# Deferred transposes for rows of scales, other PSUM banks for one projection, and moved attention steps in a two-block transformer kernel

## The chip, the cores and the metric

The kernel runs on one core of a Trainium2 chip. A core has five engines with instruction queues of their own: PE (TensorE, matmuls and transposes), DVE (VectorE), ACT (ScalarE), POOL (GpSimd) and SP (which issues DMAs here). Each works through its queue in order and waits on semaphores for the others. Matmuls write to PSUM, which has eight banks per partition; everything else lies in SBUF. The metric is the device time of one execution in microseconds, the median of several runs.

## The reference

Two transformer blocks of two layers each run one after the other on one sequence of 256 tokens with 1024 features. All of it is in float32.

```
# first block: layer 0 is attention with a forget gate, layer 1 latent attention
for layer in range(2):
    h = rms_norm(x, norm_mix_g[layer])
    x = x + (fox_mixer(h, ...) if layer == 0 else mla_mixer(h, ...))
    x = x + square(relu(rms_norm(x, norm_ffn_g[layer]) @ w_up)) @ w_down
    if layer == 0: k_nope, k_rope, v = mla_shared_kv(x, ...)   # low-rank keys and values
x = rms_norm(x, final_norm_g)
# second block: gated linear attention, then a short convolution
for i in range(2):
    h = rmsnorm(x, norm_mix_g_2[i])
    x = x + (gla_mixer(h, ...) if i == 0 else short_conv_mixer(h, ...))
    x = x + conv_ffn(rmsnorm(x, norm_ffn_g_2[i]), ...)          # silu(conv(a)) * conv(u)
x = rmsnorm(x, final_norm_g_2)

# fox_mixer: 16 heads of 64, causal; cum = cumsum(log_sigmoid(h @ w_f + b_f))
p = softmax(mask(q @ k.T / 8 + cum[query] - cum[key])); ctx = p @ v; out = ctx @ w_out
# gla_mixer: 4 heads, chunks of 64; q and k scaled by exp of cumulated log gates
scores = tril((q * exp(b)) @ (k * exp(-b)).T); o = scores @ v + (q * exp(b)) @ state
```

## The kernel before

**Split products.** Every product with a weight is made of three fp32r matmuls: activations and weights are each split into a high part and the rest, and `hh*wh + hh*wl + hl*wh` is summed in one PSUM bank (`mm3`, all recorded at L339). ACT casts a raw weight tile to `wh` (L294), DVE subtracts it to give `wl` (L312); such a pair is a *unit* of two rows of 128 by 512, made up to four units ahead of its use, in a ring of five buffers. For an activation ACT casts `hh` and DVE subtracts `hl` (L509 and L512 for norm inputs, L732 and L733 for a head pair's context).

**Ticks and what hangs on them.** The builder writes the projections one after the other and counts a tick after every group of matmuls (three of 512 columns, or six of 256; about 0.65 us). `after(n, fn)` puts a piece of other work off by n ticks, with most n in the table `DLY`. A side generator, `attend`, issues the attention visits between the groups. Its tables `FOX` and `MLA` have one entry per step: the ticks to wait, then the visits to weigh (p times v), to transpose (`pT`), and to start (logits, mask and maximum on DVE at L716, exponentials on ACT at L697; the normalisation at L704 and L707 follows eight ticks later or when the transposes need it). A fox visit is one pair of heads over all 256 queries, 8 in all; visits 4 to 7 read the second half of q, k and v. A scheduler then sets the final order of each engine's queue.

**Banks.** PSUM is parted into four accumulator banks (`acc`), three working banks (`up`) and one for transposes (`tp`); each pool is a ring. Before the output projection of fox attention needs all four accumulators, its visits borrow `acc` banks; after that (`late` is True) they take `up` banks.

**Rows of scales.** A projection whose result stands transposed (features on partitions) needs the norm's scales along the free axis. `make_row` (L137 to L149) makes such a row: DVE spreads two columns wide (L144), PE transposes them into the `tp` bank (L523), ACT copies that to `rowb` (L148). DVE's `by_row` (L416, and L419 with a factor) then multiplies the projection by it when it empties the bank.

**Linear attention.** `gla` projects v and the gate inputs, then keys (into `acc` banks), queries (into `up` banks), gates `g` (into `up` banks). While the gates' projection runs, the side generator `core` starts with the scores, which PE forms out of qT and kT; DVE multiplies the decays into qT at L1240, one half of the heads at a time.

## Time and profile before

| | |
|---|---|
| runs | 1104.15, 1104.34 and 2274.76 us; median 1104.34 us |
| the profiled execution | 1104.49 us, of which the span of instructions is 1102.7 us |
| busy share of the span | PE 99%, weight loads 91%, DVE 73%, ACT 55%, POOL 3% |
| mean granted TensorE clock | 0.997 |
| DMA | 207.3 MB, 188 GB/s in the mean |

The page gives the busy time of each engine, the span in 40 slices, the chain of work that ended last, and the costliest groups of instructions. The other views are taken from the same trace: a timeline lists an engine's instructions with the start, the length and, in brackets, an idle time ahead of them with what ended it; the waits view sums such idle times. Lines are those of the kernel before. In the changed kernel they are five higher behind `make_row` (in which L144 becomes L145 and L148 becomes L151), so that L339 there is L344, L419 is L424, and so on.

### The profile page before, as it was taken

To read this page: it belongs to the slowest core of one execution; us is meant where nothing else is said; L and a number is where in the kernel's file an instruction comes from. 1 tells how busy PE (TensorE), PEld (TensorE's weight loads), DVE (VectorE), ACT (ScalarE), POOL (GpSimd) and SP (SyncE) were. 2 spreads that over 40 slices of the span, in tenths; PEclk is the share of its full clock that TensorE was granted. 3 is DMA by queue.
4 is the path that set the end of the run, shared out by engine and by line. 5 is a ranking of instruction groups with operands and counts; after the bars stand their busy time and mean duration, and the time that the engine had idled before them with its cause. 6 is when DMAs were issued, how large, how long until landed. Compare 5 with 4: busy or idle time off the path is not lost.

```text
span 1102.7 us, 19201 instructions
## 1 busy us (share of the span) xinstructions
PE 1087.3 (99%) x7769; PEld 1003.4 (91%) x7769; DVE 801.4 (73%) x1200; ACT 609.2 (55%) x927; POOL 30.4 (3%) x55
## 2 busy tenths in 40 slices
PE   9999999999999999999999999999999999999997
PEld 7987999999988999999897899999999999999996
DVE  6687756556687766555788578787787768987786
ACT  6466655445665555545664556555555446565563
POOL 1000000000000000000010000000000000000001
PEclk9999999999999999999999999999999999999998
DMA  9844466655563566665555354566665664657551
GB/s 335 298 165 145 162 195 206 210 193 173 142 207 128 172 192 204 206 200 192 194 180 183 108 178 155 179 197 217 201 220 193 197 204 153 189 194 224 188 166 74
DMA packets 137801, 207.30 MB, mean 188 GB/s; under 512 B 10528, under 2 KB 65008, under 8 KB 137712
## 3 DMA queue, kind: packets, MB, share of 16 engines
q1 hardware_dynamic: 136576, 203.89, 56.8%
q10 hardware_dynamic: 1136, 2.17, 0.5%
q8 instruction: 61, 1.00, 0.4%
q14 instruction: 28, 0.23, 0.1%
HBM read 204.97 MB, written 1.07 MB: 187 GB/s over the span
## 4 chain that ended last, share of the span: by engine, by line
PE 87%; DVE 7%; ACT 2%; DMA 1%; issue 1%; SPq 0%; ACTq 0%; DVEq 0%
PE up L339 52%; PE acc L339 33%; DVE wl L312 2%; DMA raw<-fox_w_in 1%; ACT wh L294 1%; PE acc L523 1%; PE tp L523 1%; ACT p L697 1%; DVE p L716 1%; DVE x L602 0%; DVE p L707 0%; PE tp L533 0%; DVE tmp L1365 0%; DVE pT L725 0%; DVE kT L1232 0%
## 5 line engine op out<-in xcount | busy, mean ns | idle before, releaser
L312 DVE TENSOR_TENSOR wl<-raw,wh 128x1024 fp32r<-128x1024 f32 (+2 forms) x373 | 452.3, 1219 | 223.4 <-ACT wh L294 222.4
L294 ACT CAST wh<-raw 128x1024 fp32r<-128x1024 f32 (+2 forms) x373 | 388.8, 1043 | 381.7 <-PE up L339 253.1
L339 PE MATMUL up<-hh,wh 128*128 128x256 f32 x1564 | 431.7, 276 | 0.0
L339 PE MATMUL up<-hh,wl 128*128 128x256 f32 x1564 | 430.1, 275 | 0.0
L339 PE MATMUL up<-hl,wh 128*128 128x256 f32 x1564 | 429.4, 275 | 0.0
L339 PEld LDWEIGHTS up<-hh,wh 128*128 128x128 f32 x1564 | 300.1, 192 | 2.9 <-issue 1.5
L339 PEld LDWEIGHTS up<-hh,wl 128*128 128x128 f32 x1564 | 300.1, 192 | 0.9
L339 PEld LDWEIGHTS up<-hl,wh 128*128 128x128 f32 x1564 | 299.8, 192 | 0.3 <-DVE hl L512 0.2
L339 PE MATMUL acc<-wh,hh 128*128 128x512 f32 (+1 forms) x606 | 227.4, 375 | 0.2 <-DVE mx L716 0.2
L339 PE MATMUL acc<-wh,hl 128*128 128x512 f32 (+1 forms) x606 | 225.1, 371 | 0.1
L339 PE MATMUL acc<-wl,hh 128*128 128x512 f32 (+1 forms) x606 | 224.8, 371 | 0.0
L339 PEld LDWEIGHTS acc<-wh,hl 128*128 128x128 f32 x606 | 114.5, 189 | 15.4 <-DVE hl L1374 0.5
L339 PEld LDWEIGHTS acc<-wh,hh 128*128 128x128 f32 x606 | 114.6, 189 | 15.0 <-DVE mx L716 0.6
L339 PEld LDWEIGHTS acc<-wl,hh 128*128 128x128 f32 x606 | 114.7, 189 | 13.4
L1365 DVE SCALAR_TENSOR_TENSOR tmp<-tmp,vecs,tmp 128x255 f32<-128x255 f32 x192 | 78.0, 479 | 15.2 <-ACT tmp L1363 15.2
L339 PE MATMUL up<-wh,hh 128*128 128x512 f32 (+4 forms) x142 | 52.2, 370 | 1.8 <-DVE tmp L419 1.8
L339 PE MATMUL up<-wl,hh 128*128 128x512 f32 (+4 forms) x142 | 49.9, 352 | 0.2 <-DVE wl L312 0.2
L339 PE MATMUL up<-wh,hl 128*128 128x512 f32 (+4 forms) x142 | 49.8, 353 | 0.1
L1363 ACT ACTIVATE tmp<-tmp,vecs 128x256 f32<-128x256 f32 x96 | 40.9, 496 | 0.0
L1373 ACT CAST hh<-tmp 128x512 fp32r<-128x512 f32 x58 | 34.1, 619 | 8.3 <-DVE tmp L1418 8.3
L1374 DVE TENSOR_TENSOR hl<-tmp,hh 128x512 fp32r<-128x512 f32 x58 | 38.3, 685 | 0.0
L339 PEld LDWEIGHTS up<-wh,hh 128*128 128x128 f32 x142 | 26.8, 189 | 8.1 <-issue 5.5
(205 smaller groups left out, 769.8 us busy)
## 6 DMA issues: line engine op xcount, KB each, us to landing
raw<-ffn_w_up SPq DMA_DIRECT2D x176, 256.0 KB, 4.2
raw<-ffn_w_up SPq DMA_DIRECT2D x32, 1024.0 KB, 5.3
raw<-ffn_w_down SPq DMA_DIRECT2D x32, 1024.0 KB, 5.0
raw<-ffn_w_down SPq DMA_DIRECT2D x44, 512.0 KB, 6.6
raw<-sc_w_in SPq DMA_DIRECT2D x12, 1024.0 KB, 5.3
raw<-fox_w_in SPq DMA_DIRECT2D x10, 1024.0 KB, 9.7
raw<-gla_w_in SPq DMA_DIRECT2D x10, 1024.0 KB, 5.0
raw<-fox_w_out SPq DMA_DIRECT2D x4, 1024.0 KB, 5.2
```

The costliest lines, as they stand in the source:

```text
L294: self.last_hi = nc.scalar.copy(hi[:, :kn, :w], self.raws[r][:, k:k + kn])
L312: self.last_wl = nc.vector.tensor_tensor(out=u.lo[:, :kn, :w], in0=self.raws[r][:, k:k + kn], in1=u.hi[:, :kn, :w].bitcast(F32), op=ALU.su ...
L339: self.nc.tensor.matmul(out, lhsT, rhs, start=start, stop=stop, skip_group_check=True)
L523: self.nc.tensor.transpose(tp[:, i * P:(i + 1) * P], src[:, i * P:(i + 1) * P], self.ident)
L697: self.nc.scalar.activation(out=p[:, o:o + n], in_=p[:, o:o + n], func=AF.Exp, scale=scale, bias=nm[:, j:j + 1], accum_out=sm[:, j:j + 1])
L716: self.nc.vector.tensor_tensor_reduce(out=p[:, o:o + n], in0=lgs[h][:, w], in1=bias(h)[:, w], scale=1.0, scalar=NEG, op0=ALU.add, op1=ALU. ...
L1363: nc.scalar.activation(out=out, in_=z, func=AF.Copy, scale=w[:, 2:3])
L1365: nc.vector.scalar_tensor_tensor(out=out[:, d:], in0=z[:, :S - d], scalar=w[:, 2 - d:3 - d], in1=out[:, d:], op0=ALU.mult, op1=ALU.add)
L1373: nc.scalar.copy(hi, src)
L1374: nc.vector.tensor_tensor(out=lo, in0=src, in1=hi.bitcast(F32), op=ALU.subtract)
```

## The change

Four things are edited. `make_row` still issues the DVE copy at once, but puts the two transposes and the ACT copy off by three ticks; a set `asked` keeps a row from being made twice. `gla` projects the queries into accumulator banks. In `FOX` the first gap is 6 instead of 8, the seventh 6 for 5, the eighth 5 for 4, the ninth 7 for 5; in `MLA` the seventh is 6 for 7 and the last 3 for 2. In `DLY`, entry 0 (from the gain's multiplication of a norm input to its split) is 4 for 5, entry 1 (from an addition to x to the transposes of the next norm's input) 5 for 4, and entry 6 (the cumulation of the forget gates) 8 for 6.

```diff
--- before.py
+++ after.py
@@ -121,7 +121,7 @@
 
 
     def __init__(self, kb, tile):
-        self.kb, self.tile, self.ok, self.rows = kb, tile, set(), {}
+        self.kb, self.tile, self.ok, self.rows, self.asked = kb, tile, set(), {}, set()
 
     def set(self, *cols):
         self.ok.update(cols)
@@ -134,24 +134,29 @@
         self.wait(i[1].start, i[1].stop)
         return self.tile[i]
 
-    def make_row(self, c, tp=None):
-
-        if c in self.rows:
+    def make_row(self, c, tp=None, gap=3):
+
+        if c in self.asked:
             return
+        self.asked.add(c)
         kb, nc = self.kb, self.kb.nc
         self.wait(c, c + 2)
         wide = kb.tmp_tile()
         nc.vector.tensor_copy(wide[:, :S].rearrange("p (t n) -> p t n", t=2),
                               self.tile[:, c:c + 2].unsqueeze(2).to_broadcast([P, 2, P]))
-        tp = kb.transpose4(wide, 2, tp if tp is None else lambda: tp)
-        row = kb.small.tile([P, S], F32, tag="rowb", name=kb.name("rowb"), bufs=2)
-        nc.scalar.copy(row, tp[:, :S])
-        self.rows[c] = row
+
+        def turn():
+            bank = kb.transpose4(wide, 2, None if tp is None else lambda: tp)
+            row = kb.small.tile([P, S], F32, tag="rowb", name=kb.name("rowb"), bufs=2)
+            nc.scalar.copy(row, bank[:, :S])
+            self.rows[c] = row
+
+        kb.after(gap, turn)
 
     def row(self, c, n=2):
 
         while c not in self.rows:
-            if c in self.ok and c + 1 in self.ok:
+            if c in self.ok and c + 1 in self.ok and c not in self.asked:
                 self.make_row(c)
             else:
                 self.kb.force()
@@ -1344,7 +1349,7 @@
             self.after(DLY[21], lambda: self.prep(yy, t, list(range(4 * j, 4 * j + 4)), [(y, None)]))
 
         self.proj_T(h, 8, ev_k, self.acc_tile)
-        self.proj_T(h, 8, ev_q)
+        self.proj_T(h, 8, ev_q, self.acc_tile)
         while self.q:
             self.force()
         self.side = core()
@@ -1682,14 +1687,14 @@
 
 
 
-FOX = [(8, [], [], [0]), (6, [], [], [1]), (6, [], [0], [2]), (6, [0], [1], [3]), (6, [1], [2], [4]), (6, [2], [3], [5]),
-       (5, [3], [4], [6]), (4, [], [5], [7]), (5, [4], [6], []), (5, [5], [7], []), (5, [6], [], []), (2, [7], [], [])]
+FOX = [(6, [], [], [0]), (6, [], [], [1]), (6, [], [0], [2]), (6, [0], [1], [3]), (6, [1], [2], [4]), (6, [2], [3], [5]),
+       (6, [3], [4], [6]), (5, [], [5], [7]), (7, [4], [6], []), (5, [5], [7], []), (5, [6], [], []), (2, [7], [], [])]
 MLA = [(0, [], [], [0]), (4, [], [], [1]), (7, [], [0], []), (5, [0], [1], []), (3, [1], [], [2]), (4, [], [], [3]),
-       (7, [], [2], []), (4, [2], [3], []), (2, [3], [], [])]
+       (6, [], [2], []), (4, [2], [3], []), (3, [3], [], [])]
 
 WARM = (10, 3)
 
-DLY = [5, 4, 11, 2, 2, 3, 6, 4, 6, 2, 11, 4, 6, 2, 6, 8, 5, 1, 1, 2, 2, 5, 1, 3, 2, 1, 3, 4, 8, 2, 2, 2, 1, 1, 1, 1]
+DLY = [4, 5, 11, 2, 2, 3, 8, 4, 6, 2, 11, 4, 6, 2, 6, 8, 5, 1, 1, 2, 2, 5, 1, 3, 2, 1, 3, 4, 8, 2, 2, 2, 1, 1, 1, 1]
 
 
 @with_exitstack
```

The order of the instructions on POOL and SP is the same in both kernels. On the others it differs in many places, three of which are shown. First DVE's queue behind the masked logits of visit 3, before the change (`nm` is the shift of that visit, `rc` and `p` its normalisation, `kT_206` the second half of the keys):

```order
L794 SCALAR_TENSOR_TENSOR nm_923<-mx_918,ctok 128x4 [waits DVE_49]
L795 TENSOR_TENSOR nm_923<-nm_923,ctok 128x4 [waits DVE_49]
L312 TENSOR_TENSOR wl_938<-raw_594,wh_937 128x2x512 [waits Activation_49]
L416 TENSOR_TENSOR kT_206<-up_751,rowb_285 128x512 [waits PE_49]
L704 RECIPROCAL rc_1035<-sm_926 128x4 [waits Activation_49]
L416 TENSOR_TENSOR kT_206<-up_752,rowb_285 128x512 [waits PE_49]
L707 TENSOR_SCALAR p_917<-p_917,rc_1035 128x128 [waits DVE_49]
L707 TENSOR_SCALAR p_917<-p_917,rc_1035 128x256
L707 TENSOR_SCALAR p_917<-p_917,rc_1035 128x128
L707 TENSOR_SCALAR p_917<-p_917,rc_1035 128x256
```

And the same place now:

```order
L799 SCALAR_TENSOR_TENSOR nm_911<-mx_906,ctok 128x4 [waits DVE_49]
L800 TENSOR_TENSOR nm_911<-nm_911,ctok 128x4 [waits DVE_49]
L709 RECIPROCAL rc_1029<-sm_914 128x4 [waits Activation_49]
L712 TENSOR_SCALAR p_905<-p_905,rc_1029 128x128 [waits DVE_49]
L712 TENSOR_SCALAR p_905<-p_905,rc_1029 128x256
L712 TENSOR_SCALAR p_905<-p_905,rc_1029 128x128
L712 TENSOR_SCALAR p_905<-p_905,rc_1029 128x256
L317 TENSOR_TENSOR wl_944<-raw_594,wh_943 128x2x512 [waits Activation_49]
L421 TENSOR_TENSOR kT_206<-up_757,rowb_334 128x512 [waits PE_49]
L421 TENSOR_TENSOR kT_206<-up_758,rowb_334 128x512 [waits PE_49]
```

The two evacuations of the keys stood around the reciprocal; they now stand behind the whole normalisation and a `wl`.

The second place is PE's queue at visit 7, the last to start. Before, with the transposes of visit 5 ending and the logits in `acc` banks:

```order
L533 MATMUL tp_1198<-ident,p_1087 128x64
L533 MATMUL acc_1199<-ident,p_1087 128x64
L339 MATMUL acc_1214<-kT_206,qT_204 128x128
L339 MATMUL acc_1215<-kT_206,qT_204 128x128 [waits DVE_49]
L339 MATMUL acc_1214<-kT_206,qT_204 128x256
L339 MATMUL acc_1215<-kT_206,qT_204 128x256
L339 MATMUL acc_1234<-wh_975,hh_890 128x512 [waits DVE_49]
L339 MATMUL acc_1234<-wl_976,hh_890 128x512
L339 MATMUL acc_1234<-wh_975,hl_891 128x512
L339 MATMUL acc_1235<-wh_975,hh_890 128x512 [waits DVE_49]
```

Now (`up_1212` takes half of the transposes, `up_1227` and `up_1228` the logits of the two heads; the first group of the output projection, `acc_1197`, stands just ahead of these rows):

```order
L538 MATMUL tp_1211<-ident,p_1084 128x64
L538 MATMUL up_1212<-ident,p_1084 128x64
L344 MATMUL up_1227<-kT_206,qT_204 128x128 [waits Activation_49]
L344 MATMUL up_1227<-kT_206,qT_204 128x256
L344 MATMUL acc_1198<-wh_1020,hh_878 128x512
L344 MATMUL acc_1198<-wl_1021,hh_878 128x512
L344 MATMUL up_1228<-kT_206,qT_204 128x128 [waits Activation_49]
L344 MATMUL up_1228<-kT_206,qT_204 128x256
L344 MATMUL acc_1198<-wh_1020,hl_879 128x512
```

The logits of the two heads are now parted by matmuls of the output projection, and each of them waits for ACT. What ACT has to do there, now (`up_1018` and `up_1019` hold the two token blocks of the second half of v; the exponentials are those of visit 6):

```order
L621 ACTIVATE v_208<-up_1018,rs_117 128x512 [waits PE_49]
L702 ACTIVATE p_1159,sm_1168<-p_1159,nm_1165 128x128 [waits DVE_49,Activation_49]
L702 ACTIVATE p_1159,sm_1168<-p_1159,nm_1165 128x256
L702 ACTIVATE p_1159,sm_1168<-p_1159,nm_1165 128x128
L702 ACTIVATE p_1159,sm_1168<-p_1159,nm_1165 128x256
L621 ACTIVATE v_208<-up_1019,rs_117 128x512 [waits PE_49]
```

In the kernel before, the same six operations stand in the same order. The bank of `up_1228` is the one that `up_1019` held.

The third place is PE's queue at the end of the queries' projection in linear attention, before:

```order
L339 MATMUL up_6213<-hh_5862,wl_6177 128x256
L339 MATMUL up_6213<-hl_5863,wh_6176 128x256
L339 MATMUL up_6338<-wh_6214,hh_5748 128x512 [waits Activation_49]
L339 MATMUL up_6338<-wl_6215,hh_5748 128x512 [waits DVE_49]
L339 MATMUL up_6338<-wh_6214,hl_5749 128x512
L339 MATMUL up_6339<-wh_6214,hh_5748 128x512 [waits DVE_49,PE_49]
L339 MATMUL up_6339<-wl_6215,hh_5748 128x512
L339 MATMUL up_6339<-wh_6214,hl_5749 128x512
```

And now, up to the first scores (`up_6361`):

```order
L344 MATMUL acc_6213<-hh_5862,wl_6177 128x256
L344 MATMUL acc_6213<-hl_5863,wh_6176 128x256
L344 MATMUL up_6338<-wh_6214,hh_5748 128x512 [waits Activation_49]
L344 MATMUL up_6338<-wl_6215,hh_5748 128x512 [waits DVE_49]
L344 MATMUL up_6338<-wh_6214,hl_5749 128x512
L344 MATMUL up_6339<-wh_6214,hh_5748 128x512 [waits PE_49]
L344 MATMUL up_6339<-wl_6215,hh_5748 128x512
L344 MATMUL up_6339<-wh_6214,hl_5749 128x512
```

Eight rows further on:

```order
L344 MATMUL up_6361<-qT_5765,kT_5766 64x64 [waits DVE_49,PE_49,Activation_49]
L344 MATMUL up_6361<-qT_5765,kT_5766 64x64 x3
L344 MATMUL up_6338<-wh_6244,hh_5748 128x512 [waits Activation_49]
L344 MATMUL up_6338<-wl_6245,hh_5748 128x512
L344 MATMUL up_6361<-qT_5765,kT_5766 64x64 [waits DVE_49]
L344 MATMUL up_6361<-qT_5765,kT_5766 64x64 x3
L344 MATMUL up_6338<-wh_6244,hl_5749 128x512
```

The queries' own rows name `acc` banks, and the start of the second gate bank (`up_6339`) waits for no DVE instruction any more. The scores stand nine matmuls behind that start in both kernels, with the same waits.

## Rows read from the trace of the kernel before

**Rows 1.** The page: span, and busy time of TensorE (share of the span).

```profile
span 1102.7 us, 19201 instructions
...
PE 1087.3 (99%) x7769; PEld 1003.4 (91%) x7769; DVE 801.4 (73%) x1200; ACT 609.2 (55%) x927; POOL 30.4 (3%) x55
```

**Rows 2.** The page: the chain that ended last, its shares by engine.

```profile
PE 87%; DVE 7%; ACT 2%; DMA 1%; issue 1%; SPq 0%; ACTq 0%; DVEq 0%
```

**Rows 3.** Timeline of PE around 590: start us, duration us, engine, line, operation, [wait].

```profile
590.25 0.28 PE L339 MATMUL up<-hl,wh 128*128 128x256 f32 x1
590.37 0.38 PE L339 MATMUL up<-wh,hh 128*128 128x512 f32 x1
...
590.80 0.38 PE L339 MATMUL up<-wh,hl 128*128 128x512 f32 x1
592.93 0.45 PE L339 MATMUL up<-wh,hh 128*128 128x512 f32 x1 [1.75 <-DVE tmp L419]
...
595.04 0.45 PE L339 MATMUL up<-qT,kT 128*64 128x64 f32 x8
...
596.05 0.45 PE L339 MATMUL up<-qT,kT 128*64 128x64 f32 x8
```

**Rows 4.** Timeline of DVE in the same stretch.

```profile
589.76 2.36 DVE L312 TENSOR_TENSOR wl<-raw,wh 128x1024 fp32r<-128x1024 f32 x2
592.03 1.08 DVE L419 SCALAR_TENSOR_TENSOR tmp<-up,rowb 128x256 f32<-128x256 f32 x3
593.03 0.69 DVE L1240 TENSOR_TENSOR qT<-tmp,qT 128x512 f32<-128x512 f32 x1
...
593.96 1.22 DVE L312 TENSOR_TENSOR wl<-raw,wh 128x1024 fp32r<-128x1024 f32 x1
595.09 0.69 DVE L1240 TENSOR_TENSOR qT<-tmp,qT 128x512 f32<-128x512 f32 x1
```

**Rows 5.** Timeline of PE at the first row copy and at visits 4 and 7.

```profile
21.66 0.44 PE L523 MATMUL tp<-ident,tmp 128*128 128x128 f32 x2 [0.44 <-DVE tmp L144]
...
75.22 0.87 PE L339 MATMUL acc<-kT,qT 64*128 64x128 f32 x8
...
91.10 0.27 PE L533 MATMUL tp<-ident,p 64*128 64x64 f32 x1 [0.64 <-DVE pT L725]
...
93.62 0.48 PE L339 MATMUL acc<-wh,hh 128*128 128x512 f32 x1 [0.20 <-DVE mx L716]
```

**Rows 6.** Timeline of DVE during the visits.

```profile
64.03 0.28 DVE L716 CUSTOM_DVE_ANT_0 p<-acc,bias 128x128 f32<-128x128 f32 x1
...
73.21 0.68 DVE L416 TENSOR_TENSOR kT<-up,rowb 128x512 f32<-128x512 f32 x1
...
...
74.82 1.00 DVE L707 TENSOR_SCALAR p<-p,rc 128x128 f32<-128x128 f32 x4
75.73 1.22 DVE L312 TENSOR_TENSOR wl<-raw,wh 128x1024 fp32r<-128x1024 f32 x1
...
77.67 0.28 DVE L716 CUSTOM_DVE_ANT_0 p<-acc,bias 128x128 f32<-128x128 f32 x1
...
90.96 0.28 DVE L716 CUSTOM_DVE_ANT_0 p<-acc,bias 128x128 f32<-128x128 f32 x1
```

**Rows 7.** Timeline of PE in latent attention.

```profile
316.00 0.41 PE L523 MATMUL acc<-ident,tmp 128*128 128x128 f32 x2 [0.42 <-DVE tmp L144]
...
358.90 0.45 PE L339 MATMUL up<-pT,v 128*128 128x256 f32 x1 [0.50 <-DVE pT L725]
```

**Rows 8.** Timeline of DVE in latent attention.

```profile
355.93 2.36 DVE L312 TENSOR_TENSOR wl<-raw,wh 128x1024 fp32r<-128x1024 f32 x2
358.20 0.55 DVE L725 COPY pT<-tp 128x384 f32<-128x384 f32 x1
```

**Rows 9.** Timeline of ACT at visit 6: first exponential, and the evacuation of v.

```profile
92.64 0.40 ACT L697 ACTIVATE p<-p,nm 128x128 f32<-128x128 f32 x1 [2.10 <-DVE nm L795]
...
94.41 0.67 ACT L616 ACTIVATE v<-up,rs 128x512 f32<-128x512 f32 x1
```

## The prediction

> **What bounds the kernel now.** I read the page first. TensorE is busy for 1087.3 of 1102.7 us [rows 1], and the chain of work that ended last is 87% PE, 7% DVE and 2% ACT [rows 2]. So PE is the bound nearly everywhere, and a change that only reorders work can win no more than what PE stands still. That is 15.4 us in all, 1.4% of the time, a part of it start-up that this change does not touch. The matmuls themselves stay the same in number and shape. What counts, then, is single waits: I read the views of waits of PE and the timelines of PE, DVE and ACT in the stretches that the edits touch, and held the order of the changed program against them. The profiled execution took 1104.49 us, 0.15 over the median of 1104.34, so the two are one number here.
>
> In the timelines a reader is to see how far a PE row starts after the one ahead of it. A 256-wide matmul takes PE 0.11 us and a 512-wide one 0.215 when nothing is in the way (590.25 to 590.37, and the two from 590.37 to 590.80, in [rows 3]). Anything beyond that is a wait.
>
> **Linear attention's queries in accumulator banks.** Today the gate projection needs two `up` banks, the queries hold two of the three, and PE waits 1.75 us for DVE's L419 to empty one: the start goes from 590.80 to 592.93, 2.13 us where 0.21 would do, 1.9 lost [rows 3]. In accumulator banks the queries hold no `up` bank, and the order shows that the second gate bank no longer waits for DVE. The accumulators are empty early enough: DVE's order has their evacuation (L1200) well ahead of the wl that the queries' projection needs. So this wait goes. But what is late next? Three gate groups on, PE's scores read qT, which L1240 writes in two halves. DVE runs without a pause from 589.76 (two wl, then L419, L1240, L419, another wl, the second L1240), and ends the second half at 595.09 + 0.69 = 595.78 [rows 4]. Its order there is the same after the change. PE does the second half of the scores at 596.05 today [rows 3]. It would reach that point about 594.1, wait 0.6 us at the first half (ready 593.03 + 0.69 = 593.72) and some 1.3 us at the second, and go on at about 595.8. So of 1.9 us only 0.25 is left as gain. Just ahead, the row copy of the norm and one `hl` come later in PE's order, which spares PE up to about half a microsecond and lets the DVE chain start that much sooner, since it is fed by PE's projections; I take 0.45 of it. Together -0.7, with ends at -0.25 (no head start for DVE) and -2.4 (the wait goes in full).
>
> The Trainium skill ("Perfetto Trace Analysis", section "Optimizing Tensor Performance", Matmuls) says that independent groups of matmuls should rotate through different PSUM banks, so that the evacuation of one overlaps the matmuls of the next. By that rule the 1.9 us would all be won, and the sum would be 1.65 lower. The row agrees that the bank is what is waited for today, but it shows nothing of what comes after; the DVE rows say that the data are late too.
>
> **Rows of scales three groups later.** `make_row` now emits only the DVE copy, and its two transposes and ACT copy come three groups on. Nothing is added to any engine but two or three small rows. Where PE waited for the copy it no longer does. At 316.00 in the latent-attention layer a transpose waited 0.42 us for L144 [rows 7]; the order has it now behind the rotary transposes, and the row is wanted only when kT is evacuated, later still in DVE's order, so I take -0.45 (bounds -0.6 and 0, should the kT evacuation come to wait for the row). At 21.66, at the start, PE waited 0.44 us for L144 [rows 5]; there the head transposes of the first queries move up in its place, and they wait for ACT. I count +0.25 there, because they end no sooner. If ACT were in time the 0.44 would be a gain; both ends are small.
>
> **Latent attention's table.** The seventh gap goes from 7 to 6 and the last from 2 to 3: the third visit's transposes come one group earlier, and the weighing after them stays. Today PE waits 0.50 us at 358.90 for the pT copy [rows 7], which DVE starts at 358.20 behind two wl [rows 8]. Now the transposes come three 512-wide matmuls, 0.65 us, sooner, and in DVE's order the copy stands ahead of the second wl, so it ends 1.1 us earlier. The wait goes: -0.55 with the step from one kind of matmul to the next.
>
> **Forget-gate attention's table** is the large item. Visits 0 to 3 come 12 matmuls of 0.11 us, 1.34 us, earlier in PE's order, visits 4 and 5 three earlier, the last four steps three groups later. But a visit is a chain over DVE and ACT: four masked rows with their maxima (ISA in the order, 1.1 us), two small ones for the shift (0.4), four exponentials on ACT (1.8: 92.64 to 94.41 [rows 9]), a reciprocal and four normalisations (1.15), a wl (1.15), hl and pT (0.8): 6.65 us, which is the period between 77.67 and 90.96 [rows 6] (two periods). That chain, not PE, sets visits 4 to 7.
>
> - Visit 2's masked rows start at 64.03 now [rows 6]. Their logits come 1.34 us earlier, but DVE is full there with masks, qT and wl, and I put them at 63.05.
> - To visit 3: hl, pT and a wl all stand between, about 6.9 us: 69.95.
> - To visit 4: today DVE does the two kT evacuations from 73.21 on, before the normalisations at 74.82 and the wl at 75.73 [rows 6]. Now both stand behind reciprocal, normalisations and wl: kT is ready at about 76.2 and 76.8. PE gets to visit 4's logits at about 74.5 (75.22 before [rows 5]) and waits some 1.6 us. The chain needs 7.85: 77.8 (77.67 before).
> - To visit 5 one wl more stands ahead of the shift: 7.7, 85.5. To visit 6: 6.65, 92.15, where it was 90.96 [rows 6]. The chain is 1.2 late.
> - Visit 7: PE waited 0.64 for pT at 91.10 and 0.20 for an accumulator at 93.62 [rows 5]. A group of the output projection now stands ahead of the transposes, and the logits have `up` banks of their own, since the switch `late` is already set: both waits go. But the second logits bank is the one that holds the second half of v, and ACT empties it (L616) behind the exponentials of visit 6, at 94.41 + 0.67 today [rows 9], so at about 95.6 + 0.67 = 96.3. PE would be there at about 93.6 and waits 2.7 us.
>
> Behind that wait PE has done two matmuls (0.43 us) more than at 93.62 before, and an estimated 0.35 us of logits follow (half of a visit's, from the 0.87 of its eight rows at 75.22): 96.3 + 0.35 - 0.43 - 93.62 = **+2.6 us**. The earlier waits, the +0.25 of the start among them, are swallowed in it, as PE waits here for the chain. Bounds: if DVE keeps visit 6 at its old time, +1.4; if the 1.34 us of head start carries through, about 0; if the chain is a further 1 us late, +3.6. I take 2.6, as every DVE duration in it is from a row.
>
> The last four steps come later, so the last context parts do too: by my times the last hl ends about 0.4 us before PE reads it. This costs nothing while that holds.
>
> **Norm inputs.** With DLY[0] 4, DLY[1] 5 the transposes of x come one group later and the splits as much earlier after them. DVE's adds and hl end when they did, and that is what PE waits for at the five norm places; I count 0 (bounds -0.5 and +0.3). DLY[6], the cumulation two groups later, stands at the same place in PE's order: 0.
>
> **Sum.** +2.6 (visits, with the start) - 0.45 (row) - 0.55 (latent) - 0.7 (linear attention) = +0.9 on 1104.49: 1105.4, and on the median of 1104.34 **1105.2 us**. That is no change: a measurement of this kernel can tell about 2%, 22 us, from no change.
>
> **Rivals.**
> - *The bank was all* (chance 0.2): qT is ready sooner than I think, because DVE's chain starts sooner. The whole 1.9 and the 0.45 are won: 1105.2 - 1.65 = 1103.55. For it speaks that the chain is fed by PE; against it that DVE has no pause in [rows 4].
> - *The visits gain* (0.25): the head start of visits 0 to 3 outlives the extra wl and kT rows on DVE, and v's bank is empty 1.2 to 2.6 us sooner. Then the visits cost between +1.4 and 0: 1104.0 to 1102.6, middle 1103.3. With the bank as well, 1101.6. Against it: the order puts kT behind the normalisations.
> - *The tail breaks* (0.15), the one on the slower side: the last part of the context is late. It decides when the chain is more than 0.4 us later than I have it; each further microsecond is then a wait ahead of the last matmuls of the output projection, besides the one for v's bank. With the chain 1 us late: +1 at v's bank and +0.6 in the tail, 1106.8.
> - My forecast has 0.4: 1104.1 to 1106.2.
>
> The range, 1101.8 to 1107.0, takes in all four but for the far ends: both gaining rivals at once below it, a tail over 1 us late above it. Faster by over 2% would need more than all of PE's 15.4 us, 0.01; slower by over 2%, 22 us of new waits where I find 5, 0.01; the rest is 0.98.
>
> **What would show it.** Right: PE waits at the score matmuls (`up<-qT,kT`) near 593 to 596 for L1245, not for L424; a wait near 74 to 76 at `acc<-kT,qT` for L421; one of 2 to 3 us near 93 to 96 at `up<-kT,qT`, with ACT's L621 behind the exponentials; no wait at the pT weighing near 358 nor at L528 near 315. Wrong: visit 6's masked rows at or before 91, no wait at 74, or scores that start at 594 without a wait. What would upset the total is a new wait in the repeated layers, where I count none.

## The result and the profile after

The changed kernel takes **1110.38 us** (median of five runs, 1108.69 to 1112.18) where the kernel before takes 1104.31 (median of five): a ratio of 1.0055 with an interval of 1.0044 to 1.0067, or 6.1 us more. That is no change by the bound of 2%, but it is outside the range that was given (1101.8 to 1107.0), and nearly seven times the +0.9 that was forecast. The profiled execution took 1110.24 us, against 1104.49 before, 5.75 more.

The page of the changed kernel, the lines that answer to [rows 1] and [rows 2]:

```profile
span 1108.5 us, 19206 instructions
...
PE 1089.9 (98%) x7769; PEld 1005.5 (91%) x7769; DVE 801.5 (72%) x1200; ACT 609.4 (55%) x927; POOL 30.4 (3%) x55
...
PE 86%; DVE 9%; ACT 2%; issue 1%; DMA 1%; POOL 0%; SPq 0%; ACTq 0%; DVEq 0%; POOLq 0%
```

The matmuls are the same 7769. PE stands still for 18.6 us instead of 15.4, and it is *busy* for 2.6 us longer, which the same matmuls should not be. The second is the unusual part: these 2.6 us are not waits.

The view of PE's waits, whole kernel (engine, line, who is waited for: us in total, times, longest):

```profile
PE up L344 <- DVE hl L517: 2.5, 3, 1.4
PE up L344 <- DVE qT L1245: 1.6, 2, 0.9
...
PE acc L344 <- DVE kT L421: 1.3, 1, 1.3
PE up L344 <- ACT v L621: 1.3, 1, 1.3
```

The waits of before for the bank [rows 3] and for L144 [rows 5, 7] are gone from it. In their place stand waits for `qT`, `kT` and `v`, which were forecast, and at the top one for `hl`, which was not.

Since both kernels do the same matmuls, one can ask at each point how much later the changed kernel reaches the same amount of matmul work. I call this the **lag**; it is worked out from the starts of all 7769 matmuls of both traces, and tells where the time goes. Times of the kernel before are on the left:

| stretch (us of before) | lag at its start and end | change | forecast |
|---|---|---|---|
| start, first row copy, to 58 | 0 to -0.4 | -0.4 | } |
| forget-gate visits, 58 to 122 | -0.4 to +4.1 | +4.5 | } +2.6 |
| latent attention, 295 to 400 | +4.1 to +3.7 | -0.4 | -1.0 |
| norm input of linear attention, 535 to 570 | +3.7 to +5.5 | +1.8 | 0 |
| linear attention, 570 to 620 | +5.5 to +5.3 | -0.2 | -0.7 |
| three norm places behind it, near 653, 831, 918 | +5.3 to +5.8 | +0.45 | 0 |

The sum, +5.8, is the difference of the two profiled executions. (The lag does not move in the stretches left out.) Two more norm places lie inside these stretches, near 121 (0.17 of the second line) and near 375 (0.12, which the third line's gain has to make good). Two things make the miss: the start and the visits together reach +4.0 ahead of the norm place at 121, some 1.4 us more than was forecast, and the norm input of linear attention, counted at nothing, cost 1.8.

**The visits.** The timelines of PE, DVE and ACT, with one wait ahead of visits 4 and 7 (start us, duration, engine, line, operation, [wait]):

```profile
59.22 0.35 PE L344 MATMUL up<-hh,wh 128*128 128x256 f32 x1 [0.72 <-DVE rc L709]
...
75.81 0.93 PE L344 MATMUL acc<-kT,qT 64*128 64x128 f32 x8 [1.33 <-DVE kT L421]
...
93.87 0.38 PE L344 MATMUL acc<-wl,hh 128*128 128x512 f32 x1
95.53 1.31 PE L344 MATMUL up<-kT,qT 64*128 64x128 f32 x4 [1.28 <-ACT v L621]
96.77 0.79 PE L344 MATMUL acc<-wh,hl 128*128 128x512 f32 x1
97.36 0.63 PE L344 MATMUL acc<-wh,hh 128*128 128x512 f32 x1
97.79 0.63 PE L344 MATMUL acc<-wl,hh 128*128 128x512 f32 x1
98.21 0.63 PE L344 MATMUL acc<-wh,hl 128*128 128x512 f32 x1
98.64 0.63 PE L344 MATMUL acc<-wh,hh 128*128 128x512 f32 x1
99.07 0.52 PE L344 MATMUL acc<-wl,hh 128*128 128x512 f32 x1
99.42 0.38 PE L344 MATMUL acc<-wh,hl 128*128 128x512 f32 x1
```

```profile
75.08 1.28 DVE L421 TENSOR_TENSOR kT<-up,rowb 128x512 f32<-128x512 f32 x2
```

```profile
94.81 0.67 ACT L621 ACTIVATE v<-up,rs 128x512 f32<-128x512 f32 x1
```

Both forecast waits are there, and a third at 59.22 that the forecast does not have. The third costs little in this execution: the lag is -0.36 at 58 and -0.26 at 64. By the starts, PE stands 1.5 us for `kT` at 75.81, and 1.45 at 95.53 for the bank of `v` (from 93.87 to 95.53 is 1.66 us, where 0.215 would do). But behind the second wait the matmuls of 512 columns start 0.43 us apart (97.36, 97.79, 98.21, 98.64, 99.07) and not 0.215 as in [rows 3]. The view by windows says why (window: sum, busy of PE, PEld, DVE, ACT, POOL, granted TensorE clock as a share, DMA):

```profile
92.00:94.00 2.00, 2.00 (x20) 1.19 (x18) 1.44 (x8) 0.95 (x5) 0.00 (x0) 1.00 0.95 289
94.00:96.00 2.00, 0.72 (x5) 0.47 (x4) 1.02 (x7) 2.00 (x7) 0.00 (x0) 0.98 0.53 204
96.00:98.00 2.00, 2.00 (x6) 1.17 (x5) 1.57 (x9) 0.79 (x2) 0.41 (x1) 0.50 0.00 0
98.00:100.00 2.00, 2.00 (x7) 1.65 (x7) 1.07 (x2) 0.16 (x1) 0.72 (x2) 0.67 0.04 8
100.00:102.00 2.00, 2.00 (x11) 1.75 (x10) 1.08 (x1) 2.00 (x7) 0.00 (x0) 1.00 0.00 0
```

TensorE's granted clock fell to 0.50 behind the wait, that is to 1.2 GHz, its lower level, near 95.9, and was back at 2.4 near 99.3 (worked out from the 0.98 and the 0.67 of the windows at its two ends). The logits and the six matmuls behind them take 3.89 us from 95.53 to 99.42, where 2.2 would do at the full clock (0.85 for the logits and 0.32 for the matmul behind them, as the same rows take in a trace without the fall, and five of 0.215): 1.65 us more. This is the greater part of the 2.6 us of extra busy time.

**The norm input of linear attention.** PE's rows, and then DVE's queue, after:

```profile
550.53 0.38 PE L344 MATMUL up<-wh,hl 128*128 128x264 f32 x1 [0.61 <-DVE hl L517]
...
559.89 0.38 PE L344 MATMUL up<-wh,hl 128*128 128x264 f32 x1 [1.41 <-DVE hl L517]
```

```profile
557.93 1.30 DVE L1141 TENSOR_SCALAR x<-x,rs 128x512 f32<-128x512 f32 x3 [1.14 <-POOL rs L568]
559.16 0.68 DVE L517 TENSOR_TENSOR hl<-tmp,hh 128x512 fp32r<-128x512 f32 x1
```

and DVE's queue there before:

```profile
552.02 0.68 DVE L512 TENSOR_TENSOR hl<-tmp,hh 128x512 fp32r<-128x512 f32 x1
...
554.17 1.31 DVE L1136 TENSOR_SCALAR x<-x,rs 128x512 f32<-128x512 f32 x3 [0.86 <-POOL rs L563]
```

Before, the last `hl` stood ahead of the scaling of x, and DVE's wait for POOL's norm statistic cost nothing. Now `hl` stands behind the scaling; DVE waits 1.14 us for POOL and scales for 1.3 before it writes the `hl` that PE has been waiting for.

**Linear attention.** The bank wait of [rows 3] is gone, and the scores wait for `qT` instead, where before they did not wait:

```profile
599.39 0.45 PE L344 MATMUL up<-qT,kT 128*64 128x64 f32 x8 [0.74 <-DVE qT L1245]
...
601.37 0.45 PE L344 MATMUL up<-qT,kT 128*64 128x64 f32 x8 [0.89 <-DVE qT L1245]
```

**Latent attention.** The 0.42 us for the row copy [rows 7] is gone, and this came a little later, a wait for the split of a norm input:

```profile
321.24 0.38 PE L344 MATMUL up<-hl,wh 128*128 128x256 f32 x1 [0.52 <-DVE hl L517]
```

### The profile page after: what moved, and what is told of

It is laid out like the page before. It is cut to its first block, busy times and chain, and to the rows that moved or that the text cites. A ratio compares the mean times of both kernels' runs of the same rounds, so it can differ in the third digit from the quotient of the medians.

```text
span 1108.5 us, 19206 instructions
## 1 busy us (share of the span) xinstructions
PE 1089.9 (98%) x7769; PEld 1005.5 (91%) x7769; DVE 801.5 (72%) x1200; ACT 609.4 (55%) x927; POOL 30.4 (3%) x55
## 4 chain that ended last, share of the span: by engine, by line
PE 86%; DVE 9%; ACT 2%; issue 1%; DMA 1%; POOL 0%; SPq 0%; ACTq 0%; DVEq 0%; POOLq 0%
PE up L344 50%; PE acc L344 33%; DVE wl L317 3%; PE acc L528 1%; DMA bias<-rows 1%; ACT wh L299 1%; ACT p L702 1%; DVE p L721 1%; PE tp L528 1%; DVE p L712 0%; DVE hl L517 0%; DVE x L607 0%; DVE tmp L1370 0%; ACT tmp L621 0%; PE acc L1612 0%
## 5 line engine op out<-in xcount | busy, mean ns | idle before, releaser
L344 PE MATMUL up<-hh,wh 128*128 128x256 f32 x1532 | 423.1, 276 | 0.7 <-DVE rc L709 0.7
L344 PE MATMUL up<-hl,wh 128*128 128x256 f32 x1532 | 420.9, 276 | 0.5 <-DVE hl L517 0.5
L344 PE MATMUL up<-hh,wl 128*128 128x256 f32 x1532 | 420.8, 275 | 0.0
L344 PEld LDWEIGHTS up<-hh,wh 128*128 128x128 f32 x1532 | 294.0, 192 | 4.3 <-issue 2.4
L344 PEld LDWEIGHTS up<-hh,wl 128*128 128x128 f32 x1532 | 294.0, 192 | 0.9
L344 PEld LDWEIGHTS up<-hl,wh 128*128 128x128 f32 x1532 | 293.6, 192 | 1.1 <-DVE hl L517 0.9
L1370 DVE SCALAR_TENSOR_TENSOR tmp<-tmp,vecs,tmp 128x255 f32<-128x255 f32 x192 | 78.0, 478 | 15.4 <-ACT tmp L1368 15.4
```

The lines of the kernel that those rows point to most:

```text
L344: self.nc.tensor.matmul(out, lhsT, rhs, start=start, stop=stop, skip_group_check=True)
L1370: nc.vector.scalar_tensor_tensor(out=out[:, d:], in0=z[:, :S - d], scalar=w[:, 2 - d:3 - d], in1=out[:, d:], op0=ALU.mult, op1=ALU.add)
```

## The experiments

Two questions were open: what the visits cost without the rest (and whether the fall of the clock belongs to them), and whether the norm inputs alone make the wait for `hl`. Each part was therefore done alone or undone. Medians of the kernel before beside these runs were 1104.28 in the first two sets (27 and 30 runs) and 1104.42 in the third (21).

### The visits alone, and the change without them

`fox_only` is the kernel before with the new table of the visits:

```diff
-FOX = [(8, [], [], [0]), (6, [], [], [1]), ... (5, [3], [4], [6]), (4, [], [5], [7]), (5, [4], [6], []),
+FOX = [(6, [], [], [0]), (6, [], [], [1]), ... (6, [3], [4], [6]), (5, [], [5], [7]), (7, [4], [6], []),
```

> The kernel before with the new table of forget-gate visits (FOX) and nothing else of the change. Theory A (the table alone builds the waits for kT near 74 and for v's bank near 94, and TensorE's granted clock then falls behind the second one as in the changed kernel's trace): +4.4 us, about 1108.7, with the PE interval of 512-wide matmuls doubled for some 2 us after the wait near 94. Theory B (the waits are the table's, but the fall of the clock needs the other edits too): +2.2, about 1106.5, no slow stretch.

Measured: 1107.82 us (six runs, 1106.58 to 1108.48), ratio 1.0031 (1.002 to 1.0043). The same kernel was run again in the third set, as `fox_again`:

> The kernel before with the new FOX table, once more, beside the next run on the same chip: the spread of its executions is looked for. Theory A (behind the 1.45 us wait for v's bank TensorE's granted clock falls in some executions and not in others): two clusters, near 1107.0 and 1.2 to 1.5 us higher. Rival (the spread is noise): one cluster within 0.9 us, as the kernel before has.

Measured: 1108.23 (1107.0, 1107.03, 1108.23, 1108.43, 1108.65), ratio 1.0032 (1.0019 to 1.0044). The eleven runs of this one program fall into two groups: five at 1106.58 to 1107.56, six at 1108.09 to 1108.65. Both profiles are of the lower group. The wait for `v` is the same there as after the whole change, but no fall follows:

```profile
94.34 0.38 PE L339 MATMUL acc<-wl,hh 128*128 128x512 f32 x1
96.01 0.92 PE L339 MATMUL up<-kT,qT 64*128 64x128 f32 x4 [1.29 <-ACT v L616]
96.86 0.48 PE L339 MATMUL acc<-wh,hl 128*128 128x512 f32 x1
97.18 0.38 PE L339 MATMUL acc<-wh,hh 128*128 128x512 f32 x1
```

```profile
94.00:96.00 2.00, 0.72 (x3) 0.30 (x2) 0.55 (x3) 2.00 (x9) 0.00 (x0) 1.00 0.77 297
96.00:98.00 2.00, 1.99 (x9) 1.55 (x10) 1.97 (x13) 1.26 (x2) 0.33 (x1) 1.00 0.00 0
```

From 90 to 114 the lag rises by 1.05 in `fox_only` and in `fox_again`, and by 2.7 in the changed kernel: the fall costs 1.65, as in the rows above. At 114 it stands at +2.8, where the changed kernel's is +4.0, which is 1.2 more and not 1.65, because the changed kernel came to 90 with 0.45 less: the wait near 59 is 0.72 there, and 1.27 and 0.86 in the two profiles here. The upper group lies 1.3 above the lower (means of 1108.34 and 1107.04). So the forecast of +2.6 was right for an execution without the fall, and the fall adds 1.3 by the groups and 1.65 by the rows.

That the upper group are executions with a fall is inferred, since no profile fell on one. Besides the size, the mean granted clock of each execution speaks for it. In all 78 executions of the kernel before it is 0.997 to 0.999. The two traces with a fall (the changed kernel's and that of `best2`, below) have 0.996, and so have twelve more executions of all kernels here, each in the upper group of its kernel. The six of the upper group here have 0.9968 in the mean, the five of the lower 0.9978. Single values, rounded to 0.001, do not part the groups: five of the six show 0.997. Of the changed kernel's five executions the shortest, 1108.69, has 0.998 and the others 0.996 or 0.997, so it is likely one without a fall; at 4.4 above the kernel before it too lies outside the forecast range. So neither theory of `fox_only` came out as it stood: the table alone makes the waits, and the fall, if it is what parts the groups, comes in some executions only.

`no_fox` is the changed kernel with the old table of visits:

> The changed kernel with the old FOX table. Theory A: 4.3 us of the 6 go, about 1106.0, and no slow stretch of TensorE before 110 us. Rival (the waits only move to the output projection of this layer or later): more than 1108.

Measured: 1106.56 (eleven runs, 1105.58 to 1108.0), ratio 1.0023 (1.0014 to 1.0032). The lag is +0.2 at 295, -0.2 at 535, +1.6 at 570 and +1.6 at the end. By the medians the visits make 3.8 of the 6.1 us; the rest of the change costs 2.3 us where I had it gain 1.7. The profiled execution, at 1106.09, is 0.5 below the median; the three longest, 1107.54 to 1108.0, are at a granted clock of 0.996, so a fall, which this kernel's waits for `qT` can bring as well (see `best2`), is likely in them. The old visits with entry 6 of `DLY` at 8 leave the lag at 0 from 58 to 118, so that entry cost nothing there.

### Visit 7 with the old banks

`fox_v7` is the changed kernel with visit 7 started one group earlier, when it still takes its logits from accumulator banks, so that nothing waits for `v`:

```diff
-       (6, [3], [4], [6]), (5, [], [5], [7]), (7, [4], [6], []), ...
+       (6, [3], [4], [6]), (4, [], [5], [7]), (7, [4], [6], []), ...
```

> The changed kernel with the eighth gap of FOX 4 in place of 5: visit 7 starts a group earlier, while its logits still have accumulator banks, so nothing waits for the bank that holds the second half of v. Theory A (that wait, and the fall of the clock behind it, are the dearest part of the table): no wait near 94 and no slow stretch there, 2.7 us less than the changed kernel, about 1107.7; the 1.5 us for kT near 74 stay. Rival (the softmax chain on DVE and ACT sets the end of the layer whatever bank is used): within 0.7 of 1110.4.

Measured: 1107.37 (eight runs, 1106.86 to 1107.71), ratio 1.0026 (1.0016 to 1.0036): 3.0 us less than the changed kernel for one number. The waits of PE between 55 and 125 are these, without `v`:

```profile
PE acc L344 <- DVE kT L421: 1.4, 1, 1.4
PE up L344 <- DVE nm L800: 1.2, 1, 1.2
```

The granted clock is 1.00 in every window from 92 to 102, and the runs lie within 0.9 us instead of in two groups. From 90 to 114 the lag falls by 0.9, where it rises by 1.05 in `fox_only` (the late bank, no fall) and by 2.7 in the changed kernel (both). So by the traces the late bank costs 1.9 us, of which 1.45 are the wait itself, and the fall behind it another 1.65. That is 3.6 where the medians differ by 3.0; in the profiles 0.8 of it is not seen at the end, since `fox_v7` came to 90 with that much more lag (its wait near 60 is 1.2 us and not 0.72, and its start 0.3 later).

### A longer occupation of the bank

To see whether a longer wait makes the fall certain, `fox_long` adds to `fox_only` one more evacuation of the same bank by ACT, into a scratch tile, ahead of that of `v`:

```diff
             def f(t, ps):
+                if t:
+                    junk = self.small.tile([P, 512], F32, tag="junk", name=self.name("junk"), bufs=1)
+                    self.scaled(junk, ps, rs[:, t:t + 1])
                 self.scaled(v[i][:, t], ps, rs[:, t:t + 1])
```

> The same with one more evacuation of v's second block on ACT (into a scratch tile, used by nobody) ahead of the one that PE waits for: the wait for v's bank grows by 0.57 us to about 2.0. Theory A (a longer wait makes the fall of the clock the rule): +0.6 by the wait and the upper cluster in most executions, median near 1109. Rival (the fall does not hang on this wait): +0.6 on the median of the run beside it and the same spread.

Measured: 1108.56 (1106.82, 1107.3, 1108.56, 1108.95, 1109.07), ratio 1.0036 (1.0022 to 1.005). This decides nothing. The bank came free later, but the order had moved and PE did two more matmuls first, so that it stood idle for 1.45 us by the timeline instead of 1.29, and the groups are as before (two executions at 1106.82 and 1107.3 with a granted clock of 0.997 and 0.998, three at 1108.56 to 1109.07 with 0.996).

### The norm inputs

`dly01_only` is the kernel before with entries 0 and 1 of `DLY` changed:

```diff
-DLY = [5, 4, 11, ...
+DLY = [4, 5, 11, ...
```

> The kernel before with DLY[0] 4 and DLY[1] 5 and nothing else. Theory A (the second low half of the linear attention's input then stands in DVE's queue behind operations that wait for POOL's norm statistics): a wait of about 1.4 us at the hl matmul near 555 and one of 0.6 near 547, +1.8 there and +0.1 at each later norm: about 1106.3. Rival (the later row copy makes that wait): within 0.4 of 1104.3.

Measured: 1106.71 (ten runs, 1105.97 to 1107.21), ratio 1.0023 (1.0014 to 1.0032), so **+2.4 us** from a term that was counted at 0. Its waits between 540 and 570, where the kernel before has none on PE:

```profile
PE up L339 <- DVE hl L512: 2.0, 2, 1.4
```

The lag goes from +0.5 at 535 to +2.15 at 570, then in steps of 0.17 near 653, 831 and 918: the three late steps of the changed kernel are here too, as are those near 121 (0.17) and 375 (0.12).

`dly0_only` changes entry 0 alone:

> The kernel before with DLY[0] 4 (splits one group sooner after the gain) and the transposes of x where they were. Theory A (the loss of the pair is the transposes' later place, which puts the last hl behind DVE operations that wait for POOL): no loss, the 0.3 us wait for hl near 552 goes, about 1103.9. Rival (the sooner split is what reorders DVE): 1106 or more.

Measured: 1105.65 (eleven runs, 1105.43 to 1105.92), ratio 1.0011 (1.0002 to 1.002), +1.4. My theory, that the earlier split alone would do no harm, fell. DVE's order had turned over with that entry alone:

```profile
554.30 1.31 DVE L1136 TENSOR_SCALAR x<-x,rs 128x512 f32<-128x512 f32 x3 [1.14 <-POOL rs L563]
555.53 0.68 DVE L512 TENSOR_TENSOR hl<-tmp,hh 128x512 fp32r<-128x512 f32 x1
```

This `hl` stood at 552.02 before, ahead of the scaling. Of the 2.4 us, 1.4 are thus entry 0; the rest comes with entry 1, as a second wait for `hl` near 547 and the five steps of 0.12 to 0.17 at the other norm places, of which entry 0 alone shows none.

### The rows of scales

`row_only` is the kernel before with the new `make_row`:

> The kernel before with the deferred transposes of rows and nothing else. Theory A (what is won at 304, 315 and 557, 0.15 + 0.58 + 0.2, is partly paid back by a wait of 0.7 for an hl in latent attention): -0.2, about 1104.1. Rival (the rows' waits simply go): -0.9, 1103.4.

Measured: 1104.88 (eleven runs, 1104.45 to 1105.1), ratio 1.0005 (0.9996 to 1.0013): +0.6, inside the interval, where I had -0.45 at 316 and +0.25 at the start. Neither theory of the run (-0.2 and -0.9) came out. At 316 the wait for L144 is gone, and one for the split takes its place:

```profile
316.80 0.38 PE L344 MATMUL up<-hl,wh 128*128 128x256 f32 x1 [0.53 <-DVE hl L517]
```

which leaves no gain: the lag is -0.51 at 315 and -0.51 at 318. A gain of 0.2 stands a little ahead, near 304, at the row for the latent queries, which the forecast did not count. Between 554 and 600 the row of linear attention, moved back, lays open a wait, beside the one for L424's bank that it does not touch:

```profile
PE up L344 <- ACT v L621: 0.5, 1, 0.5
```

```profile
557.39 0.48 ACT L621 ACTIVATE v<-up,rs 128x264 f32<-128x264 f32 x1 [2.18 <-POOL rs L1137]
```

The bank that the next matmuls need holds a piece of v, which ACT empties only when POOL's norm statistic is there. In the kernel before the row's transposes stood at this place (557.90) and now they come at 559.98. The lag goes from -0.5 to +0.2. So one of the rows gains 0.2 and one costs 0.7. What the start costs is not shown: the lag rises by 0.2 at the first row, where PE now waits 0.7 for ACT as forecast, but at the same place it moves by -0.2 to +0.6 in kernels that do not have this edit.

### The queries' banks

`accq_only` is the kernel before with the queries in accumulator banks:

```diff
-        self.proj_T(h, 8, ev_q)
+        self.proj_T(h, 8, ev_q, self.acc_tile)
```

> The kernel before with the linear attention's queries in accumulator banks and nothing else. Theory A (the scores wait for qT on DVE in place of the bank): -0.25, about 1104.05, with waits for L1240 of about 0.7 and 0.9 at the scores. Rival (the bank was all): -1.9, about 1102.4, no wait at the scores.

Measured: 1104.19 (eleven runs, 1103.73 to 1105.73), ratio 1.0002 (0.9994 to 1.0011). The 1.75 us for the bank have turned into this, between 554 and 600:

```profile
PE up L339 <- DVE qT L1240: 1.6, 2, 0.9
```

The lag shows -0.25 from this edit (-0.05 to -0.3), which is the size worked out for it without the head start of 0.45. Three of the eleven runs lie at 1105.5 to 1105.7 (granted clock 0.996 and 0.997), 1.6 above the mean of the others. `best2`, below, has the same edit, and its profile shows what such a run can be.

### Combinations

`best1` takes the rows, the queries' banks and the latent table, and leaves the visits and `DLY` as they were. `best2` is the same, but only the row of column 2 is put off, the others are made at once as before:

```diff
+        if c == 2:
+            kb.after(gap, turn)
+        else:
+            turn()
```

`best3` is `best2` without the banks.

> The changed kernel with the old FOX table and the old DLY: deferred rows, queries in accumulator banks, the new MLA table. Theory A (the three are worth -0.2, -0.25 and -0.4): about 1103.4, beats both kernels by little. Rival (waits at the scores bring a fall of the clock in some executions, as the spread of the run with the banks alone hints): median at or above 1104.3, with single runs 1.5 above the others.

> The kernel before with the new MLA table, queries in accumulator banks, and deferred transposes for the rows of column 2 alone (latent queries and short convolution), the other rows at once. Theory A: -0.55 for latent attention's table, -0.2 for the row at 304, -0.25 for the banks: 1103.3, but a fall of the clock at the scores in some executions, 1.5 each. Rival (the gains do not add): 1104.1.

> The same without the accumulator banks: -0.55 and -0.2, 1103.5, and a spread as narrow as that of the kernel before, since no wait at the scores is made. Rival (the gains do not add): 1104.1.

Measured: `best1` 1104.16 (eleven runs, 1103.81 to 1106.44), ratio 1.0002 (0.9993 to 1.0011); `best2` 1103.66 (1103.13 to 1105.73), 0.9997 (0.9989 to 1.0006); `best3` 1103.77 (1103.56 to 1104.52), 0.9995 (0.9986 to 1.0004). Against the kernel before all three are the same; `best3` has a median 0.65 lower and no outlying run. Against the changed kernel they are 6 to 7 us faster. `best1` missed the 1103.4 of its theory: the row near 557 costs it 0.7 (lag -0.31 at 552 and +0.38 at 565), and two of its executions, 1105.77 and 1106.44, are long ones at a granted clock of 0.996. The latent table gains 0.4 in `best1` and `best3` alike (lag from +0.06 to -0.31, and from -0.45 to -0.82, between 340 and 370).

`best2`'s profiled execution, at 1104.82, was one of its long ones. Behind the second wait for `qT` the clock fell here too, from about 595.3 to 598.7:

```profile
592.83 0.45 PE L347 MATMUL up<-qT,kT 128*64 128x64 f32 x8 [0.74 <-DVE qT L1248]
593.21 0.48 PE L347 MATMUL up<-wh,hh 128*128 128x512 f32 x1
593.53 0.38 PE L347 MATMUL up<-wl,hh 128*128 128x512 f32 x1
594.81 0.45 PE L347 MATMUL up<-qT,kT 128*64 128x64 f32 x8 [0.90 <-DVE qT L1248]
...
596.96 0.63 PE L347 MATMUL up<-wl,hh 128*128 128x512 f32 x1
597.39 0.63 PE L347 MATMUL up<-wh,hl 128*128 128x512 f32 x1
```

```profile
594.00:596.00 2.00, 1.19 (x11) 0.95 (x12) 1.43 (x4) 0.00 (x0) 0.00 (x0) 0.83 0.78 304
596.00:598.00 2.00, 2.00 (x9) 1.25 (x7) 1.44 (x2) 0.59 (x1) 0.00 (x0) 0.50 0.00 0
598.00:600.00 2.00, 2.00 (x24) 1.80 (x24) 0.89 (x2) 0.00 (x0) 0.00 (x0) 0.81 0.58 144
```

Its lag goes from -1.04 at 585 to +0.36 at 600, where `accq_only`, without a fall, goes down by 0.23: the fall costs 1.6 here.

## Why the prediction was wrong, step by step

Taken alone, the parts come to +3.7 (visits, the eleven runs of `fox_only` and `fox_again` together, median 1108.09), +2.4 (norm inputs), +0.6 (rows), -0.1 (banks) and -0.4 (latent table, by the lag): +6.2, against 6.1 measured. Each can be held against its term. That the sum comes so near is partly luck: each median has an interval of about 1 us to either side, and the 0.7 that the rows cost near 557 is not in the changed kernel, where PE waits for `hl` at that place and the waits view has no wait for `v` there.

- **Norm inputs: 0 forecast (bounds -0.5 and +0.3), +2.4 measured. This step failed first.** It said that DVE's adds and `hl` "end when they did". They did not: DVE takes its queue in order, and the new delays turned over the order of the last `hl` and of a scaling that waits for POOL. The term was argued from the delays in the table and not from DVE's order at the norm places, where the turned rows could be seen in the order of the program before any run. The five other norm places add 0.12 to 0.17 each.
- **The visits: +2.6 forecast. The mechanism was right, and what comes behind a wait was left out.** The trace of the visits alone has +2.8. DVE's masked rows of visits 2 to 6 start at 62.40, 69.23, 77.07, 84.72 and 91.38, each 0.65 to 0.8 earlier than forecast (63.05 to 92.15); the wait for `kT` is 1.5 (1.6 forecast); the wait for `v` 1.45 (2.7 forecast, since `v` was empty at 95.5 and not 96.3, and PE came at 94.1 and not 93.6). Because the forecast took all earlier waits as swallowed by a longer one, its sum came out near all the same, which is luck in part; the wait near 59 is in no term. The six times given for the chain add up to 6.4 and not to the 6.65 that was used, which is the measured period; the steps themselves came out as forecast (77.07 to 84.72 is 7.65 for 7.7, 84.72 to 91.38 is 6.66 for 6.65). The missing step is the clock: a wait was priced at its own length, and behind this one TensorE ran at its lower level from 95.9 to 99.3, which cost 1.65 in the profiled execution and 1.3 between the groups of `fox_only`.
- **Rows of scales: -0.45 and +0.25 forecast, +0.6 measured.** The wait at 316 went, as forecast, and nothing was gained by it: the bound of 0 was right, by another cause than the one named, since not kT's evacuation but `hl` was late next. The start's +0.25 cannot be told from its spread. Two places were missed: the row near 304 gains 0.2, and the row near 557, taken from where it was, leaves PE to wait for a bank that ACT cannot empty yet, 0.7 in `row_only`.
- **Linear attention: -0.7 forecast, -0.2 measured.** The main step was right, the scores wait for `qT` twice, 0.74 and 0.89 where 0.6 and 1.3 were forecast, and of 1.9 us only 0.25 is left. The head start of 0.45 failed: the places from which it was to come, the row and an `hl` near 557, are those that now wait. By the rule of the Trainium skill ("Perfetto Trace Analysis", section "Optimizing Tensor Performance", Matmuls) on rotating groups through PSUM banks, the whole 1.9 would have been won; the trace does not bear this out here, where the data behind the bank are late as well.
- **Latent table: -0.55 forecast, about -0.4 measured.** The step held: the weighing no longer waits 0.5 for `pT`, and the changed kernel's lag goes from +3.97 at 350 to +3.60 at 366.
- **The rivals.** "The bank was all" fell in `accq_only`. "The visits gain" fell in `fox_only`. "The tail breaks" was on the right side, but no wait shows ahead of the last matmuls of the output projection. The side on which the result lies was thus given 0.15, for a reason that did not happen.
- **The range** gave the norm places +0.3 at most, and nothing to the clock. The last sentence of the forecast named a new wait in the repeated layers as what would upset the total, and gave it no width; what came there is 0.17 at each of three norm places.

## What to carry to other kernels

When a table of delays is edited, read the order of each in-order queue at every place that the entry touches: an operation that slips behind one that waits for a third engine inherits the whole wait (here an `hl` behind a scaling that waits 1.14 us for POOL, 1.4 us in all). When a wait is taken away, look for the next thing that is late and for what stands behind the moved work; three edits here (rows, banks, latent table) each removed the wait they were aimed at, and two of the three brought another of nearly the same size. A new stall of TensorE can cost more than its own length (here 1.45 and another 1.3 to 1.65), so look at the granted clock behind it.

## What the runs showed of the hardware

The granted TensorE clock fell to 0.50 from 95.9 to 99.3 us behind a wait of 1.45 us (changed kernel), and from 595.3 to 598.7 behind two waits of 0.9 and 1.06 us by the starts, with work between them (`best2`). It did not fall behind the same 1.45 us in `fox_only`, nor behind the 1.9 us of [rows 3], where the windows from 588 to 598 show 1.00 throughout, nor behind the 1.41 us at 559.89. The two waits for `qT`, 0.7 and 0.9 by the view, stand in the profiles of the changed kernel, `no_fox` and `accq_only` too, and there the windows around them show 1.00. The kernel before, whose longest wait past the start is the 1.9 us, has 30 runs within 1.1 us in the second set, at granted clocks of 0.997 to 0.999; so whether the clock falls is not a matter of the wait's length alone, and what else decides it stays open here. What it costs when it falls is read from the lag: 1.65 us in the changed kernel (2.7 from 90 to 114, against 1.05 without a fall) and 1.6 in `best2` (+1.4, against -0.23).

The Trainium skill ("Perfetto Trace Analysis", section "Matmul Optimizations") says that the matmul engine scales its power by how much it is used, so that matmuls should run back to back in batches. The rows agree in direction, 1.00 ahead of the wait and 0.50 behind it. The times and clocks of the single executions, and the fall in `best2`, say further that it comes in some executions and not in others.
